# Rotation tables from angles, input weights built transposed in PSUM, scan states kept in PSUM

## The chip, the core and the metric

The kernel runs on one core of a Trainium2 chip. The metric is device time in microseconds (us) of one launch: 1091.52 us, the median of three runs (1089.41 to 1093.77). The engines are TensorE (PE; its weight loads are listed as PEld), VectorE (DVE), ScalarE (ACT), GpSimd (POOL) and SyncE (SP), which here only issues DMAs.

## The reference

Two encoder layers over 256 tokens of width 1024. Layer 0 mixes tokens with a state-space layer (S5), layer 1 with dilated attention; each then attends to 256 memory tokens and ends in an MLP. The change touches S5 alone: 64 groups of 16 channels, 64 complex states each, two directions.

```python
dt = exp(log_dt);  mag = exp(lam_re * dt);  ang = lam_im * dt
abar = mag * (cos(ang) + i sin(ang));  f = (abar - 1) / lam
bu  = einsum('bsgc,gpc->bsgp', u, f * b)                 # input into the states
x_t = abar * x_(t-1) + bu_t                              # scan over 256 tokens, both ways
y   = Re(einsum('bsgp,gcp->bsgc', x, c)) + d * u         # read out, then gelu and a GLU
```

Beside it stand the memory projections, `rms_norm(mem) @ w_kv` for both layers, which need nothing from S5.

## The kernel before, in words

Four tokens make one step, so a scan has 64 steps with the factor abar^4. The 64 groups go in eight chunks of eight. A chunk's states are 128 partitions (direction, state) by 512 columns (group, step), in one PSUM bank for the real part and one for the imaginary.

`s5_load`, `s5_params`, `s5_tables`, `s5_b`, `s5_turns`, `s5_c`, `s5_input` and `s5_skip` are the pre-phase. It ends with the powers of abar (`tav`, `taq`), the transposed input `u2` and the rotations e^(i k theta) as a product of two small tables. Then `s5` runs the chunks:

- `s5_weigh_in` (L1019): six DVE products make the input weights V (L1027 to L1029), PE transposes them (L1034), ACT copies them out (L1036).
- `turn` (L1056): six POOL products (L747 to L750) make the chunk's rotation table T.
- `drive` (L1065): 32 small matmuls (64 in the trace, two passes each) put V times u into the two state banks (L1073).
- `scan` (L1079): on DVE, rotate by T (six instructions from L1088), run the real recurrence (L1097), rotate back (six from L1100). ACT copies the states to SBUF (L1108, L1109).
- `impulse` (L1124): PE builds a kernel for the four tokens of one step (L1136, L1141), which goes through DRAM and back as M (L1146, L1152, both on ACT's queue).
- `weigh_out` (L1111): six POOL products make the output weights W.
- `read` (L1155): PE multiplies states by W and inputs by M (L1162, L1164); gelu (L1166); transposes (L1170); split into two halves (L1173 on ACT, L1174 on DVE).

In chunk ch the code puts weigh-in and drive of ch+1, scan of ch, impulse of ch, read of ch-1, weigh-out of ch+1. The memory projections (`memory_part`, `gemm32`, L241) are written after `s5`, but the scheduler that builds the program lays the instructions of each engine in one fixed order, and fits them in where its model of the engines has room. Each engine runs its own order strictly. The weights of the projections (`raw`, four buffers) are loaded on SP's queue, which is also in order.

After S5 come the last memory projection, which uses weights split into high and low halves (L154 on ACT, L155 on DVE, L200 to L202 on PE), the GLU and the other stages.

Of the kernel before, what the change touches and what calls it, by code (L numbers as in the profile page):

```python
# [17 lines left out]
P = 128  # L18
D = 1024
KT = 8  # L20
S = 256
DFF = 4096
EPS = 1e-6
NEG_INF = -1e30
XH = 4
# [36 lines left out]
class Trunk:  # L62
# [18 lines left out]
    @contextmanager  # L81
    def banks(self, na, nb):

        with self.tc.tile_pool(name="pa", bufs=na, space=PSUM) as self.pa, \
                self.tc.tile_pool(name="pb", bufs=nb, space=PSUM) as self.pb:
            yield
# [11 lines left out]
    def psb(self):  # L98
        return self.pb.tile([P, 512], F32, tag="B", name="psb")

# [651 lines left out]
    def s5_params(self, pr):  # L752
# [21 lines left out]
        v.tensor_scalar(n, th, 1.0 / (2 * math.pi), 12582912.0, op0=ALU.mult, op1=ALU.add)  # L774
        v.tensor_scalar(n, n, 12582912.0, None, op0=ALU.subtract)
# [5 lines left out]
        v.tensor_scalar(th, th, 3.1415925, -3.1415925, op0=ALU.min, op1=ALU.max)  # L781
        sn, hs, cs = nt(), nt(), nt()
        nc.scalar.activation(sn, th, AF.Sin)
        last = nc.scalar.activation(hs, th, AF.Sin, scale=0.5)
        self.exp_ln(last)
        v.tensor_tensor(hs, hs, hs, op=ALU.mult)
        v.tensor_scalar(cs, hs, -2.0, 1.0, op0=ALU.mult, op1=ALU.add)
        self.disc = (nt, mag, sn, cs)

    def s5_tables(self, ph):  # L790

# [3 lines left out]
        nt, mag, sn, cs = self.disc  # L795
# [3 lines left out]
        def table(name, l, copy=v.tensor_copy):  # L799
            ps = self.psb()  # L800
# [6 lines left out]
        e, q1, q2 = nt([G, 2, 2, 64]), nt(), nt()  # L807
        src = (cs, sn)
        for i in range(2):
            v.tensor_tensor(q1, src[1], src[1], op=ALU.mult)  # L810
            v.tensor_tensor(q2, src[0], src[0], op=ALU.mult)
            v.scalar_tensor_tensor(e[:, 1], src[0], 2.0 if i == 0 else -2.0, src[1], op0=ALU.mult, op1=ALU.mult)
            v.tensor_tensor(e[:, 0], q2, q1, op=ALU.subtract)
            src = (e[:, 0], e[:, 1])
# [3 lines left out]
        self.te = table("te", [e[:, 0], e[:, 1], r4])  # L818
# [16 lines left out]
        av, aq = nt([G, 2, 4, 2, 64]), nt([G, 2, 4, 2, 64])  # L835
# [5 lines left out]
        self.tav = table("tav", rows(av))  # L841
# [16 lines left out]
    def s5_load(self, pr, mem, craw):  # L858
# [19 lines left out]
        self.gb = pr.tile([64, D], F32, tag="gb", name="gb")  # L878
        nc.sync.dma_start(self.gb, a["norm_mix"][0].partition_broadcast(64))
# [9 lines left out]
    def s5_b(self, ph):  # L889
# [6 lines left out]
        for ri in range(2):  # L896
            for c0 in (0, 8):
                ps = self.psb()
# [5 lines left out]
    def s5_c(self, ph, pr):  # L904
# [4 lines left out]
        for c0 in (0, 8):  # L909
            pss = []  # L910
            for ri in range(2):
                ps = self.psb()
# [8 lines left out]
    def s5_skip(self, ph, pr):  # L921

        nc, a = self.nc, self.a
        G = 64
        dn = pr.tile([G, 16], F32, tag="dn", name="dn")
        nc.sync.dma_start(dn, a["s5_d"][0].rearrange("(g c) -> g c", c=16))
        dr = pr.tile([G, 8, 16], F32, tag="dr", name="dr")
        nc.gpsimd.tensor_copy(dr, dn.unsqueeze(1).to_broadcast([G, 8, 16]))
        ps = self.psb()
        nc.tensor.transpose(ps[:, :G], dr.rearrange("g a c -> g (a c)"), self.ident[:G, :G])  # L930
        dc = pr.tile([P, 16], F32, tag="dc", name="dc")
        for j in range(4):
            nc.vector.tensor_copy(dc[32 * j:32 * j + 32, :], ps[32 * j:32 * j + 32, j:G:4])
# [22 lines left out]
    def s5_input(self, ph):  # L956
# [7 lines left out]
        for q in range(4):  # L964
            t = xs[q % 2]
            cs = slice(q * 256, (q + 1) * 256)
            for s in range(4):
                nc.vector.scalar_tensor_tensor(t[:, :, 0, s], self.xraw[s][:, cs].rearrange("k (g c) -> k g c", c=16),
                                               r[:, s:s + 1], self.gb[:, cs].rearrange("k (g c) -> k g c", c=16),
                                               op0=ALU.mult, op1=ALU.mult)  # L970
            nc.scalar.copy(t[:, :, 1].rearrange("k g s c -> k g (s c)"), t[:, :, 0].rearrange("k g s c -> k g (s c)"))
            for b in range(2):
                ps = self.psb()
# [4 lines left out]
                nc.scalar.copy(u[:, g0:g0 + 8, 1:65], ps.rearrange("p (g k) -> p g k", g=8))  # L978
        self.u2 = u

    def s5_turns(self, ph, early, t):

        nc = self.nc
        G = 64
        t = t.rearrange("p (r w g b) -> p r w g b", r=2, w=2, g=G)

        e = ph.tile([P, 2, 3, 2, G], F32, tag="sq", name="sq")
        v, gp = nc.vector, nc.gpsimd
        v.tensor_copy(e[:, :, 0, 0, :], self.te[:, 0:2, :])
        for i in range(5):  # L990
            (r, i0), (ro, io) = ([e[:, q, k % 3, k // 3, :] for q in range(2)] for k in (i, i + 1))
            x, y = (ph.tile([P, G], F32, tag="sqt%d" % q, name="sqt") for q in range(2))
            v.tensor_tensor(x, r, r, op=ALU.mult)
            v.tensor_tensor(y, i0, i0, op=ALU.mult)
            v.tensor_tensor(ro, x, y, op=ALU.subtract)
            v.scalar_tensor_tensor(io, r, 2.0, i0, op0=ALU.mult, op1=ALU.mult)
        fl = lambda x: x.rearrange("p w g b -> p (w g) b")
        gp.memset(t[:, 0, :, :, 0:1], 1.0)
        gp.memset(t[:, 1, :, :, 0:1], 0.0)
        for st in range(3):  # L1000
            m = 1 << st
            eb = [e[:, q, st].rearrange("p w g -> p (w g)").unsqueeze(2).to_broadcast([P, 2 * G, m]) for q in range(2)]

            def tmp():
                x = early.tile([P, 512], F32, tag="pt8", name="pt", bufs=2)
                return x[:, :2 * G * m].rearrange("p (g m) -> p g m", m=m)

            self.cmul(gp if st == 2 else v, [fl(t[:, q])[:, :, m:2 * m] for q in range(2)], [fl(t[:, q])[:, :, 0:m] for q in range(2)],
                      eb, tmp)
        return t  # L1010
# [8 lines left out]
    def s5_weigh_in(self, early, ch):  # L1019

        nc, v = self.nc, self.nc.vector
        V = early.tile([P, 8, 2, 4, 16], F32, tag="V", name="V")
        (ar, ai), (br, bn) = ([f(x, ch, ri) for ri in range(2)] for f, x in ((self.pwb, self.tav), (self.bcb, self.bb)))
        for o, (x0, y0, x1, y1, op) in ((V[:, :, 0], (ar, br, ai, bn, ALU.add)),
                                        (V[:, :, 1], (ai, br, ar, bn, ALU.subtract))):
            t0, t1 = self.tmp(early, 8, 4, 16), self.tmp(early, 8, 4, 16)
            v.tensor_tensor(t0, x0, y0, op=ALU.mult)  # L1027
            v.tensor_tensor(t1, x1, y1, op=ALU.mult)
            v.tensor_tensor(o, t0, t1, op=op)  # L1029
        VT = early.tile([P, 8, P], F32, tag="VT", name="VT", bufs=1)  # L1030
        for q in range(2):
            ps = self.psb()
            for j in range(4):
                nc.tensor.transpose(ps[:, j * P:(j + 1) * P],  # L1034
                                    V[:, 4 * q + j].rearrange("p r s c -> p (r s c)"), self.ident)
            nc.scalar.copy(VT[:, 4 * q:4 * q + 4, :], ps.rearrange("p (a b) -> p a b", a=4))  # L1036
        self.Vs[ch] = VT

    def s5(self, ph, early, turns, gT):
# [339 lines left out]
```

## Time and profile before

| | |
|---|---|
| median of three runs | 1091.52 us |
| the profiled execution | 1089.65 us |
| its span, first to last instruction | 1087.9 us |
| PE busy over the span | 1032.4 us (95%) |
| DVE, ACT, POOL busy | 723.2 (66%), 576.9 (53%), 223.0 us (21%) |
| granted PE clock, mean | 0.983 of full |

A busy share is a mean over stages with different limits. S5 takes about the first fifth of the span, so the share that matters for the change is that of its own stretches. The granted clock is in parts of 2.4 GHz; its lower level, 1.2 GHz, reads 0.5.

### The profile page before, as it was taken

To read this page: it belongs to the slowest core of one execution; us is meant where nothing else is said; L and a number is where in the kernel's file an instruction comes from. 1 tells how busy PE (TensorE), PEld (TensorE's weight loads), DVE (VectorE), ACT (ScalarE), POOL (GpSimd) and SP (SyncE) were. 2 spreads that over 40 slices of the span, in tenths; PEclk is the share of its full clock that TensorE was granted. 3 is DMA by queue.
4 is the path that set the end of the run, shared out by engine and by line. 5 is a ranking of instruction groups with operands and counts; after the bars stand their busy time and mean duration, and the time that the engine had idled before them with its cause. 6 is when DMAs were issued, how large, how long until landed. Compare 5 with 4: busy or idle time off the path is not lost. (4 is left out here: it accounts for less than half of the span.)

```text
span 1087.9 us, 16868 instructions
## 1 busy us (share of the span) xinstructions
PE 1032.4 (95%) x6526; PEld 847.5 (78%) x6526; DVE 723.2 (66%) x1101; ACT 576.9 (53%) x1026; POOL 223.0 (21%) x186
## 2 busy tenths in 40 slices
PE   4689899998999999999989999999999999999998
PEld 3445565566899899998868878878788989889996
DVE  7999998346678754445576776778836766454444
ACT  6254444375576654444445665667545656444443
POOL 3979985011000010011040030000200000100000
PEclk8799999998999999999999999999999999999999
DMA  8313223255552456655566556554434435556552
GB/s 200 86 54 108 64 76 115 90 178 176 178 175 102 134 179 190 190 180 190 177 193 174 169 159 182 162 156 137 134 116 155 136 116 168 185 174 196 188 187 104
DMA packets 98428, 164.04 MB, mean 151 GB/s; under 512 B 16640, under 2 KB 27052, under 8 KB 98092
## 3 DMA queue, kind: packets, MB, share of 16 engines
q1 hardware_dynamic: 89052, 159.10, 47.7%
q10 hardware_dynamic: 9296, 3.87, 1.4%
q8 instruction: 51, 0.84, 0.3%
q14 instruction: 29, 0.24, 0.1%
HBM read 160.96 MB, written 3.83 MB: 151 GB/s over the span
## 5 line engine op out<-in xcount | busy, mean ns | idle before, releaser
L155 DVE TENSOR_TENSOR wlo<-raw,whi 128x1024 fp32r<-128x1024 f32 x264 | 329.9, 1250 | 238.5 <-ACT whi L154 235.0
L154 ACT CAST whi<-raw 128x1024 fp32r<-128x1024 f32 x264 | 276.7, 1048 | 226.5 <-PE psa L202 142.0
L200 PE MATMUL psa<-whi,xs 128*128 128x512 f32 x448 | 177.6, 397 | 0.5 <-ACT sg L1204 0.5
L202 PE MATMUL psa<-whi,xs 128*128 128x512 f32 x448 | 176.7, 394 | 0.0
L201 PE MATMUL psa<-wlo,xs 128*128 128x512 f32 x448 | 176.3, 393 | 0.0
L285 POOL TENSOR_TENSOR sq<-rl 128x512 f32<-128x512 f32 x32 | 40.1, 1252 | 534.2 <-ACT rl L284 534.2
L272 PE MATMUL psb<-xs,whi 128*128 128x256 f32 x512 | 145.1, 283 | 0.0
L274 PE MATMUL psb<-xs,whi 128*128 128x256 f32 x512 | 145.0, 283 | 0.0
L276 PE MATMUL psb<-xs,wlo 128*128 128x256 f32 x512 | 144.9, 283 | 0.0
L202 PE MATMUL psa<-whi,hl 128*128 128x512 f32 x256 | 101.5, 397 | 0.0
L201 PE MATMUL psa<-wlo,hh 128*128 128x512 f32 x256 | 101.5, 397 | 0.0
L200 PE MATMUL psa<-whi,hh 128*128 128x512 f32 x256 | 101.4, 396 | 0.0
L272 PEld LDWEIGHTS psb<-xs,whi 128*128 128x128 f32 x512 | 98.2, 192 | 0.9 <-DVE xs L177 0.4
L274 PEld LDWEIGHTS psb<-xs,whi 128*128 128x128 f32 x512 | 98.2, 192 | 0.5
L276 PEld LDWEIGHTS psb<-xs,wlo 128*128 128x128 f32 x512 | 98.3, 192 | 0.0
L200 PEld LDWEIGHTS psa<-whi,xs 128*128 128x128 f32 x448 | 84.3, 188 | 16.8 <-ACT sg L1204 0.9
L202 PEld LDWEIGHTS psa<-whi,xs 128*128 128x128 f32 x448 | 84.2, 188 | 16.5
L201 PEld LDWEIGHTS psa<-wlo,xs 128*128 128x128 f32 x448 | 84.3, 188 | 15.9
L241 PE MATMUL psa<-raw,mT 128*128 128x512 f32 x192 | 94.6, 636 | 0.0
L241 PEld LDWEIGHTS psa<-raw,mT 128*128 128x128 f32 x192 | 36.8, 203 | 38.5 <-issue 37.5
L202 PEld LDWEIGHTS psa<-whi,hl 128*128 128x128 f32 x256 | 48.2, 188 | 11.6
L201 PEld LDWEIGHTS psa<-wlo,hh 128*128 128x128 f32 x256 | 48.3, 189 | 11.1
(332 smaller groups left out, 1630.2 us busy)
## 6 DMA issues: line engine op xcount, KB each, us to landing
raw<-in_mlp_w SPq DMA_DIRECT2D x128, 512.0 KB, 4.3
raw<-in_attn_w_qkv SPq DMA_DIRECT2D x72, 512.0 KB, 3.8
raw<-in_xattn_w_kv SPq DMA_DIRECT2D x32, 512.0 KB, 4.0
raw<-in_s_w_glu SPq DMA_DIRECT2D x16, 512.0 KB, 4.6
raw<-in_xattn_w_q SPq DMA_DIRECT2D x16, 512.0 KB, 3.4
raw<-in_xattn_w_o SPq DMA_DIRECT2D x16, 512.0 KB, 3.6
raw<-in_attn_w_o SPq DMA_DIRECT2D x8, 512.0 KB, 4.4
bias_d<-bias_o SPq DMA_DIRECT2D x1, 1536.0 KB
```

Of the source, the lines that this page charges most:

```text
L154: self.nc.scalar.copy(hi, src)
L155: self.nc.vector.tensor_sub(lo, src, hi.bitcast(F32))
L200: nc.tensor.matmul(acc[t], xh[:, k0 + k, sl], hi[:, k % 2, :], start=st, stop=False)
L201: nc.tensor.matmul(acc[t], xh[:, k0 + k, sl], lo[:, k % 2, :], start=False, stop=False)
L202: nc.tensor.matmul(acc[t], xl[:, k0 + k, sl], hi[:, k % 2, :], start=False, stop=en)
L241: nc.tensor.matmul(acc[t], xT[:, k + q, t * P:(t + 1) * P], raw[:, q, :], start=k + q == 0, stop=k + q == KT - 1)
L272: nc.tensor.matmul(o, hi[:, k % 2, fs], xh[:, kt, :], start=st, stop=False, skip_group_check=True)
L274: nc.tensor.matmul(o, hi[:, k % 2, fs], xl[:, kt, :], start=False, stop=False, skip_group_check=True)
L276: nc.tensor.matmul(o, lo[:, k % 2, fs], xh[:, kt, :], start=False, stop=en, skip_group_check=True)
L285: nc.gpsimd.tensor_mul(sq, rl, rl)
```

## The change

1. *Rotations from angles.* `s5_params` also works out theta of a step, in turns and reduced (`nf`, seven DVE instructions). `s5_turn` makes a whole table T for one chunk from it: three products on DVE (chunks 0 and 1) or POOL (2 to 7), then one Abs and two Sin on ACT. All eight tables are made in the pre-phase and kept, in the space of `h`, `k1`, `k0` and one slot. `s5_turns` and `turn` go.
2. *Input weights.* The powers `av` are written to DRAM with their negative. For each chunk eight DMAs read them back into A, each row to 16 partitions. ACT spreads b over the four tokens (E, two halves), PE transposes E into PSUM, and one DVE product per half, PSUM times A, gives both parts of V with the contraction over all 128 partitions. `drive` uses them so.
3. *States.* The second rotation ends in the PSUM banks; ACT copies from there in four pieces of 64x512.
4. *Input.* ACT scales x by the row norm and writes it twice; the gain is applied when DVE takes the transposes out of PSUM.
5. *Banks.* The pool of accumulators has two banks instead of three, the common pool two instead of five, and the states get four of their own.

```diff
+    def s5_turn(self, early, T, ch, eng):
...
+        eng.tensor_tensor(y, self.kn.unsqueeze(1).to_broadcast([P, 8, 64]),
+                          self.te[:, 1, 8 * ch:8 * ch + 8].unsqueeze(2).to_broadcast([P, 8, 64]), op=ALU.mult)
+        eng.tensor_scalar(n, y, MAGIC, MAGIC, op0=ALU.add, op1=ALU.subtract)
+        eng.tensor_tensor(T[:, 1], n, y, op=ALU.subtract)
+        nc.scalar.activation(T[:, 0], T[:, 1], AF.Abs)
+        nc.scalar.activation(T[:, 0], T[:, 0], AF.Sin, scale=-6.283185, bias=self.quarter)
+        nc.scalar.activation(T[:, 1], T[:, 1], AF.Sin, scale=-6.283185)
...
     def s5_weigh_in(self, early, ch):
...
+        A = self.A1 if ch % 2 else early.tile([P, 2, 8, P], F32, tag="A", name="A")
+        for q in range(8):
...
+            nc.sync.dma_start(A[16 * q:16 * q + 16].rearrange("c v g x -> c v (g x)"), src)
+        for h in range(2):
+            E = early.tile([P, 4, 2, 4, 16], F32, tag="E", name="E")
+            for ri in range(2):
+                nc.scalar.copy(E[:, :, ri], self.bcb(self.bb, ch, ri)[:, 4 * h:4 * h + 4])
             ps = self.psb()
             for j in range(4):
+                nc.tensor.transpose(ps[:, j * P:(j + 1) * P], E[:, j].rearrange("p r s c -> p (r s c)"),
+                                    self.ident)
+            nc.vector.tensor_tensor(V, ps.rearrange("p (g x) -> p g x", g=4).unsqueeze(1).to_broadcast([P, 2, 4, P]),
+                                    A[:, :, 4 * h:4 * h + 4], op=ALU.mult)
...
         def drive(ch):
...
-            S_ = [self.psb(), self.psb()]
+            S_ = [self.pss(), self.pss()]
...
-                                         VT[hs, j, 64 * d:64 * d + 64],
-                                         self.u2[hs, 8 * ch + j, 0:64] if d == 0 else
-                                         self.u2[hs, 8 * ch + j, 65:1:-1], start=True, stop=True)
+                                         V[j // 4][:, ri, j % 4, 64 * d:64 * d + 64],
+                                         self.u2[:, 8 * ch + j, 0:64] if d == 0 else
+                                         self.u2[:, 8 * ch + j, 65:1:-1], start=True, stop=True)
...
-            with k.banks(3, 5):
+            with k.banks(2, 2, 4):
...
+                        k.s5_turn(ph, Ts[0], 0, nc.vector)
+                        k.s5_turn(ph, Ts[1], 1, nc.vector)
                         k.s5_weigh_in(ph, 0)
                         k.s5_c(ph, pr)
+                        k.s5_skip(ph, pr)
                         k.s5_input(ph)
+                        for c in range(2, 8):
+                            k.s5_turn(ph, Ts[c], c, nc.gpsimd)
```

How the built order moves, at three places. First PE in the middle of the chunks, before: one chunk's gelu transposes, the next chunk's weight transposes and drive, and L241, the memory projections.

```order
L241 MATMUL psa<-raw,mT 128x512
L1170 MATMUL psb<-ident,G 128x64 x4
L1034 MATMUL psb<-ident,V 128x128 x8
L241 MATMUL psa<-raw,mT 128x512 x7
L1073 MATMUL psb<-u_487,VT 64x64 x32
L1136 MATMUL psb<-wk,bb 32x112 x8
```

The same place now (L1172 gelu transposes, L1047 weight transposes, L1077 drive, L1138 and L1143 impulse):

```order
L1172 MATMUL psb<-ident,G 128x64 x4
L1047 MATMUL psb<-ident,E 128x128 x8
L1077 MATMUL pss<-u_461,V 64x64 x32
L1138 MATMUL psb<-wk,bb 32x112 x8
L1143 MATMUL psb<-dd,ident 128x16
```

No projection matmul (now L249) stands between drive of chunk 0 and drive of chunk 7 any more: 16 of the 96 come ahead of the chunks, 80 after the last drive. In the trace each counts twice.

Second, SP's queue ahead of and in the chunks, before: weights of the projections.

```order
L227 DMA raw<-in_xattn_w_kv 128x2x512 x2
L926 DMA dn<-in_s_d 64x16
L476 DMA tb<-in_bias_table 32x24
L480 DMA junk<-in_bias_onehot 33x384
L227 DMA raw<-in_xattn_w_kv 128x2x512 x4
```

Now (`avd` is the DRAM copy of the powers; `A` and `v_91` are the two buffers of A):

```order
L235 DMA raw<-in_xattn_w_kv 128x2x512 x2
L858 DMA avd<-h 64x4x128 x4
L484 DMA tb<-in_bias_table 32x24
L488 DMA junk<-in_bias_onehot 33x384
L1039 DMA A<-avd 16x2x1024 x8
L1039 DMA v_91<-avd 16x2x1024 x8
```

Behind these come six more groups of eight reads, the gains and `h`, and only then the next weights.

Third, ACT in the pre-phase, before: squares of x, copies of b and the two small row norms.

```order
L951 ACTIVATE k_82,uss<-xs 64x1024 x2
L901 ACTIVATE bb<-psb 128x8x64
L130 ACTIVATE rs_l<-uss 64x4
L901 ACTIVATE bb<-psb 128x8x64
L131 ACTIVATE ur<-rs_l 64x4
```

Now, further on in the pre-phase, part of the tables (L1018 Abs, L1020 and L1021 Sin) with the norm of the memory (L138, L139) between:

```order
L1018 ACTIVATE k_87<-k_87 128x512
L138 ACT_TABLE_LOAD
L138 ACTIVATE rs_l<-ssv 128x2
L1020 ACT_TABLE_LOAD
L1020 ACTIVATE k_87<-k_87,quarter 128x512
L1021 ACTIVATE k_87<-k_87 128x512
L1018 ACTIVATE k_87<-k_87 128x512
L139 ACT_TABLE_LOAD
L139 ACTIVATE rmem<-rs_l 128x2
L1020 ACT_TABLE_LOAD
```

The two norms, which shared one function table, now change tables four times between Sin's; with those of the other norm ACT has seven loads after its first Sin where it had one. The copies of u, which ACT made at L971, are the 16 scalings of L987 now.

## Rows read from the trace of the kernel before

**Rows 1.** stretches, all engines: busy us (count), granted clock, DMA share, GB/s

```profile
0.00:67.00 67.00, 43.46 (x290) 29.17 (x291) 59.93 (x132) 32.20 (x64) 40.80 (x49) 0.82 0.54 132
67.00:189.00 122.00, 109.22 (x1108) 66.18 (x1112) 117.29 (x139) 55.82 (x105) 104.07 (x82) 0.97 0.28 84
189.00:230.00 41.00, 39.49 (x280) 22.70 (x270) 14.88 (x22) 15.91 (x28) 0.00 (x0) 1.00 0.27 79
230.00:300.00 70.00, 65.33 (x280) 52.23 (x281) 41.88 (x50) 45.73 (x85) 9.50 (x4) 0.95 0.61 197
```

**Rows 2.** line L1088 on DVE: ns min/median/max, first and last start

```profile
L1088 DVE TENSOR_TENSOR tmp<-psb,xs x8: 690/691/692, 67.0 to 189.6; 128x512 f32<-128x512 f32 x8
```

**Rows 3.** groups on DVE, 104-185 us: count, busy us, mean ns

```profile
L1029 DVE TENSOR_TENSOR V<-tmp 128x512 f32<-128x512 f32 x9 | 11.8, 1309 | 0.5
L1097 DVE TENSOR_TENSOR_SCAN psb<-R,psb 128x512 f32<-128x512 f32 x10 | 11.6, 1210 | 0.0
...
L1090 DVE TENSOR_TENSOR psb<-psb,xs 128x512 f32<-128x512 f32 x5 | 3.5, 700 | 0.5
...
L1174 DVE TENSOR_TENSOR xs<-psb,xs 128x256 fp32r<-128x256 f32 x4 | 1.6, 412 | 0.0
```

**Rows 4.** the matmuls of the memory projections on PE

```profile
L241 PE MATMUL psa<-raw,mT x192: 592/592/1220, 24.3 to 227.4; 128*128 128x512 f32 x192
```

**Rows 5.** PE in time order, 113-134 us: start us, length us

```profile
113.89 1.16 PE L1073 MATMUL psb<-u,VT 64*64 64x64 f32 x64 [2.13 <-DVE xs L1174]
114.98 0.61 PE L1136 MATMUL psb<-wk,bb 128*32 128x112 f32 x16
...
116.72 0.45 PE L1162 MATMUL psb<-W,xs 128*64 128x64 f32 x4
...
121.76 1.12 PE L241 MATMUL psa<-raw,mT 128*128 128x512 f32 x2
...
124.42 6.17 PE L241 MATMUL psa<-raw,mT 128*128 128x512 f32 x14
132.87 1.65 PE L1073 MATMUL psb<-u,VT 64*64 64x64 f32 x64 [2.27 <-DVE xt L1104]
```

**Rows 6.** ACT in order of time, 142 to 145 us

```profile
142.29 0.59 ACT L1166 ACTIVATE G<-psb 64x512 f32<-64x512 f32 x1 [2.22 <-PE psb L1164]
142.38 2.52 ACTq L1152 DMA_DIRECT2D M<-kd  x4
144.94 0.37 ACT L1173 CAST xs<-psb 128x256 fp32r<-128x256 f32 x1 [2.05 <-PE psb L1034]
```

**Rows 7.** ACT in order of time, at 10.6 us

```profile
10.57 0.84 ACT L175 ACTIVATE mT<-psb,gains 128x256 f32<-128x256 f32 x2 [0.94 <-DVE n L811]
```

**Rows 8.** groups on ACT by shape, 0 to 80 us

```profile
L175 ACT ACTIVATE mT<-psb,gains 128x256 f32<-128x256 f32 x16 | 6.1, 486 | 0.9 <-DVE n L811 0.9
L978 ACT COPY u<-psb 128x512 f32<-128x512 f32 x8 | 4.5, 584 | 6.2 <-PE psb L976 6.2
L951 ACT ACTIVATE k<-xs 64x1024 f32<-64x1024 f32 x4 | 4.2, 1052 | 0.0
L901 ACT ACTIVATE bb<-psb 128x512 f32<-128x512 f32 x4 | 4.0, 1030 | 0.0
...
L1129 ACT COPY wk<-W 64x384 f32<-64x384 f32 x3 | 1.5, 512 | 3.9 <-POOL W L1121 3.9
...
L783 ACT ACT_TABLE_LOAD x1 | 1.3, 1283 | 0.0
L1083 ACT COPY R<-te 128x512 f32<-128x512 f32 x2 | 1.3, 628 | 0.0
...
L1127 ACT COPY wk<-ct 128x256 f32<-128x256 f32 x2 | 0.8, 416 | 0.0
```

**Rows 9.** PE in order of time, where the next two stages begin

```profile
229.88 0.50 PE L200 MATMUL psa<-whi,mp 128*128 128x512 f32 x1 [1.51 <-ACT junk L483]
...
261.05 0.39 PE L200 MATMUL psa<-whi,xs 128*128 128x512 f32 x1
```

More of the change, by code (lines that the diff above doesn't have):

```diff
@@ L81, in banks @@
     @contextmanager
-    def banks(self, na, nb):
+    def banks(self, na, nb, ns=0):
         with self.tc.tile_pool(name="pa", bufs=na, space=PSUM) as self.pa, \
                 self.tc.tile_pool(name="pb", bufs=nb, space=PSUM) as self.pb:
-            yield
+            if ns:
+                with self.tc.tile_pool(name="ps", bufs=ns, space=PSUM) as self.ps:
+                    yield
+            else:
+                yield
     def exp_ln(self, after=None):
@@ L805, in table @@
             return o
[L807 to L814, printed above, removed]
         r4 = nt()
@@ L840, in s5_tables @@
         rows = lambda x: [x[:, ri, q] for ri in range(2) for q in range(4)]
-        self.tav = table("tav", rows(av))
+        dp = self.ctx.enter_context(self.tc.tile_pool(name="av", bufs=1, space=bass.MemoryType.DRAM))
+        self.avd = dp.tile([2, 2, 4, G, P], F32, name="avd")
+        nav = self.h[:G, 1, :512].rearrange("g (s x) -> g s x", s=4)
+        avf = av.rearrange("g r s d p -> g r s (d p)")
+        nc.scalar.mul(nav, avf[:, 0], -1.0)
+        to = self.avd.rearrange("v r s g x -> v r g s x")
+        for v_, r_, src in ((0, 0, avf[:, 0]), (0, 1, avf[:, 1]), (1, 0, avf[:, 1]), (1, 1, nav)):
+            nc.sync.dma_start(to[v_, r_], src)
         nr, den, f = nt(), nt(), nt([G, 2, 2, 64])
@@ L997, in s5_turns @@
[L997 to L1009, printed above, removed]
@@ L1010, in s5_turns @@
-        return t
+        self.kn = ph.tile([P, 64], F32, tag="kn", name="kn")
+        one = ph.tile([P, 64], F32, tag="one", name="one")
+        nc.vector.memset(one, 1.0)
+        nc.vector.tensor_tensor_scan(self.kn, one, one, -1.0, op0=ALU.mult, op1=ALU.add)
+        self.quarter = ph.tile([P, 1], F32, tag="quarter", name="quarter")
+        nc.vector.memset(self.quarter, math.pi / 2)
+    def s5_turn(self, early, T, ch, eng):
+        nc = self.nc
+        y, n = (early.tile([P, 512], F32, tag="pt%d" % q, name="pt", bufs=2).rearrange("p (g k) -> p g k", g=8)
+                for q in range(2))
+        eng.tensor_tensor(y, self.kn.unsqueeze(1).to_broadcast([P, 8, 64]),
[5 more added lines that the diff above has]
+        nc.scalar.activation(T[:, 1], T[:, 1], AF.Sin, scale=-6.283185)
@@ L1019, in s5_weigh_in @@
     def s5_weigh_in(self, early, ch):
[L1021 to L1029, printed above, removed]
@@ L1030, in s5_weigh_in @@
-        VT = early.tile([P, 8, P], F32, tag="VT", name="VT", bufs=1)
-        for q in range(2):
+        nc = self.nc
+        d = self.avd[:, :, :, :, :]
+        A = self.A1 if ch % 2 else early.tile([P, 2, 8, P], F32, tag="A", name="A")
+        step = 64 * P
+        for q in range(8):
+            src = bass.AP(tensor=d.tensor, offset=d.offset + q * step + 8 * ch * P,
+                          ap=[[0, 16], [8 * step, 2], [1, 8 * P]])
+            nc.sync.dma_start(A[16 * q:16 * q + 16].rearrange("c v g x -> c v (g x)"), src)
@@ L1175, in read @@
                                     op=ALU.subtract)
-        for step in (turn, drive, weigh_out):
+        for step in (drive, weigh_out):
             step(0)
```

133 lines of the change are left out of this document (62 added, 71 removed).

## The prediction

> **What bounds the kernel now.** I read the stretches first, then the DVE and PE rows of the chunks. Up to 189 us DVE is the engine that sets the pace: busy 59.9 of the first 67 us and 117.3 of the next 122 [rows 1]. The scans of chunks 0 and 7 begin at 67.0 and 189.6, so a chunk takes 122.6 / 7 = 17.5 us [rows 2]. PE is just as full there (109.2 of 122), but not with S5: between the small matmuls lie the projections, a stretch of 14 passes at a time, and PE waits for DVE only a little over 2 us before each drive [rows 5]. From 189 us DVE is nearly idle and PE is full [rows 1]: it finishes projections and the last reads, and the next stage's first matmul comes at 229.9 [rows 9]. From there on PE sets the time. So the question is when PE has done all it must do ahead of that matmul, and that depends on what lies beside what.
>
> **The order, and what it costs.** The 192 passes of L241 run from 24.3 to 227.4 us [rows 4], a dense pass every 6.17 / 14 = 0.44 us [rows 5]. That is 85 us of PE work, most of it now free beside DVE. In the new order 32 passes precede the chunks and 160 come after the last drive; during the chunks PE has nothing to fill its waits with. The weights could not come earlier anyway: they are queued on SP behind the reads of A for chunk 7, whose buffer is free only after chunk 5. I therefore work out three pieces: the start of the first scan, seven chunk periods, and what PE has left from the last scan's start.
>
> *First scan.* DVE loses much of its pre-phase, but ACT gains more, and the drive of chunk 0 is held by it: its matmuls stand among the transposes of the memory, whose two banks are freed by ACT's copies, and these stand in ACT's order behind all eight rotation tables and the copies of W. ACT begins that work at 10.6 us [rows 7]. Kept work [rows 8]: 12 copies of mT at 6.1 / 16 = 0.38, squares of x 4.2, b 4.0, squares of the memory about 2.3 (half as wide as those of x), power tables about 2: 17.1 us. New: 24 instructions of 128x512 for the tables at 0.63 = 15.1; seven table loads at 1.28 = 9.0; 16 scalings of x, priced like L978 at 0.58 = 9.3; six copies into E at 0.42 = 2.5; a negated copy 0.6; the norms under 1: 37.3. Then R 0.63 and 0.2, and wk 0.42 and 4 x 0.51: 3.3. Together 57.7, hence 68.3. I add 4 for waits (POOL makes six angles and then W of chunk 0, PE the transposes of u) and 2.5 for the drive: 75 us, 8 later than now. Without any wait it is 67 to 71; with POOL a few us slower, 82.
>
> On the loads the page and the rows differ. In this trace a load is 1.28 us and nothing else [rows 8]. The Trainium skill (ScalarE: Activation LUTs, What ACT_TABLE_LOAD costs) adds a drain of about 1.38 us to each switch; by it the seven would cost 9.7 us more and the total would be 1141. The trace does not bear the drain out, and I leave it out.
>
> *A chunk period.* DVE's own work falls. Now V takes six instructions of about 1.3 us next to POOL [rows 3]; in their place come two products of 1,024 elements with one operand in PSUM, 2.5 us at the rate of the rotations (0.70 for 512, started 0.60 apart). With the scan (12 x 0.60, 2 x 1.21 = 9.6) and the 0.41 of L1174 that is 12.5. But each pair of products stands directly ahead of its own scan, so the chain now goes through PE and ACT and back. From the end of the second product:
> - three quarters of a drive and a handover, 2.1. A drive is 64 passes; on 64x64 tiles it takes 1.16 [rows 5]. No row shows it over all 128 rows. Bounds are 1.16 below and, above, the read's four passes of 128x64 in 0.37, which make 5.9 for 64. I take 2.5, since two column halves can still run together as the four of the impulse row do.
> - impulse, 114.98 to 116.72 = 1.75, and read of the chunk before, 116.72 to 121.76 = 5.0 [rows 5]
> - gelu starts 0.15 later; from gelu's start to the cast is 2.65, because four DMA issues (2.52) stand between [rows 6]; they still do
> - cast 0.37, handover 0.15, L1174's counterpart 0.41, handover 0.15, two products 2.5. The product needs that copy: it frees the bank into which E's second half is transposed (the common pool has two banks).
>
> The sum is 15.3 at full clock. PE then has two waits per chunk, about 1 and 2.2 us. After a wait of 2.13 the drive took 1.16, after one of 2.27 it took 1.65, with the clock at its lower level [rows 5]. I add 0.3 for that: 15.6. The least is 13.5 (DVE's 12.5 and half a drive that it waits for), the most 24 (the 8.8 us of PE in the chain at 1.2 GHz). The reads of A stay hidden: eight issues at 2.52 / 4 = 0.63 [rows 6] are 5 us, and the buffer is free two chunks ahead; late reads would add up to 5 us per chunk.
>
> For the drive the Trainium skill (TensorEngine Tiling (Array Packing), Tiling Modes) allows four tiles at 64x64 and two at 128x64. By it 64 passes take 2.3 us, and the total would be 1 us less than mine; no row here shows it.
>
> *What PE has left.* From the start of the last scan: 160 passes x 0.44 = 70.4; reads of chunks 5, 6, 7, 15.1; impulse 1.75; the rest of the drive 1; three sets of gelu transposes about 1.4; bias matmuls and gain transposes about 2.5; four changes of accumulator at about 0.5, now that two banks hold just one pair: 94 us. Before, it was 229.9 - 189.6 = 40.3.
>
> *Sum.* 75 + 7 x 15.6 + 94 = 278 against 229.9: 48 us later. Some comes back. In 230 to 300 us PE has 4.7 us idle and a clock of 0.95, which is 3.5 lost over 70 us [rows 1], as key norms and weight splits on ACT come late; the next stage begins only 31.2 us after the last [rows 9]. These can now run beside the 70 us of projections. I give back 7 of 8.2. So +41 on the profiled 1089.65: 1131 us. (The median of three is 1.9 above the profiled execution, a small matter here.)
>
> **Rivals.**
> - *DVE alone counts* (the other side). If what ACT and PE gain lies hidden, the first scan could start near 40 us (ACT's 57.7 less the new 37.3, then drive) and the period be 12.5. That is 40 + 87.5 + 94 = 222, 8 us early, 15 with the later gain: 1075. It decides where the way from drive through read, gelu and cast is shorter than DVE's 12.5 and ACT is not the last of the pre-phase. For it: DVE is full now and loses a third of a chunk. Against: the sum of 15.3 holds no doubtful row but the drive, and the 94 us of tail remain.
> - *Gelu's DMA issues get out of the way*, and the pre-phase has no waits: 67 + 7 x 13.5 + 94 = 255.5, +25.6, less 8: 1107. For it: in one chunk PE waits less than in another, and ACT has room. Against: the issues follow gelu in the new order as well.
> - *The clock stays low in the chunks.* PE loses its filler; if the waits keep it at 1.2 GHz, the period is 24: 80 + 168 + 94 = 342, 112 later, less 7: 1195. For it: the drive at 132.87 [rows 5], and a clock of 0.82 in the first 67 us [rows 1], where PE has gaps. Against: a slower PE makes the gaps shorter, and after 2.13 us it was at full speed.
>
> **How the numbers follow.** The forecast has 0.62, its own range 1115 to 1152 (first scan 70 to 80, period 14.8 to 17, 3 to 8 us given back). The issues rival 0.18, the clock rival 0.11, both slower. DVE alone 0.06. Between these, no change, 0.03. A change of 0.5%, 5.5 us, is about what a measurement of this kernel can tell from none. So slower 0.91, same 0.03, faster 0.06. The range leaves out the first rival and most of the clock rival: 1100 to 1165.
>
> **What would show it.** Right: no L249 on PE between the first and the last drive; the first scan near 75 us with ACT busy before it; a period near 15.6 with DVE idle about 2.5 us per chunk, waiting for PE or for the cast; some 70 us of dense L249 behind the last scan's start; the next stage's first matmul (L208) near 278, its stretch shorter than 31.2. A drive row tells whether 2.5 was right. Wrong, if the first scan comes before 55 us or the period is under 13; if PE's clock in the chunks is near 0.5; or if the time is under 1100, which would mean that the tail of 94 us is not there.

## The result and the profile after

The changed kernel takes 1137.15 us (median of four runs, 1133.66 to 1139.9) against 1092.64 (1089.41 to 1096.59) in the same comparison: ratio 1.0404, 95% interval 1.0358 to 1.045. Forecast were 1131 us and a range of 1100 to 1165. The profiled execution took 1137.31 us, its span is 1135.5.

The stretches of the changed kernel, cut where the first scan begins, where the last one begins and where the next stage's first matmul begins, and then 70 us more (start and end, length, then busy us and count of PE, PEld, DVE, ACT, POOL; granted clock, DMA share, GB/s). They answer to [rows 1].

```profile
0.00:75.80 75.80, 46.56 (x253) 29.77 (x255) 36.46 (x87) 60.53 (x111) 51.81 (x56) 0.84 0.67 131
75.80:183.50 107.70, 79.17 (x1025) 64.12 (x1022) 86.45 (x118) 52.62 (x116) 41.26 (x37) 0.77 0.39 69
183.50:281.30 97.80, 94.89 (x395) 46.92 (x391) 17.65 (x27) 29.45 (x65) 3.75 (x2) 0.96 0.51 167
281.30:351.30 70.00, 69.53 (x313) 56.44 (x314) 42.18 (x50) 41.23 (x61) 4.73 (x2) 1.00 0.55 182
```

DVE has become light: 36 us of the first 76 and 86 of the 108 in the chunks. ACT is now the busiest engine ahead of the first scan, PE the full one behind the last. Over the chunks as a whole no engine is full, as one expects of a chain that goes from engine to engine.

The first, fifth, sixth and last start of a scan on DVE (start, length, in brackets the idle time before it and what ended it), answering to [rows 2]:

```profile
75.85 0.69 DVE L1092 TENSOR_TENSOR tmp<-pss,xs 128x512 f32<-128x512 f32 x1 [10.30 <-PE pss L1077]
...
134.87 0.69 DVE L1092 TENSOR_TENSOR tmp<-pss,k 128x512 f32<-128x512 f32 x1 [1.23 <-PE pss L1077]
151.23 0.69 DVE L1092 TENSOR_TENSOR tmp<-pss,k 128x512 f32<-128x512 f32 x1 [1.23 <-PE pss L1077]
...
183.47 0.69 DVE L1092 TENSOR_TENSOR tmp<-pss,k 128x512 f32<-128x512 f32 x1 [1.23 <-PE pss L1077]
```

So the first scan begins at 75.85 (forecast 75), and seven periods take 107.6 us, 15.4 each (forecast 15.6, before 17.5). PE around the last drive and behind it, and where the next two stages begin:

```profile
182.30 2.49 PE L1077 MATMUL pss<-u,V 128*64 128x64 f32 x44 [0.20 <-DVE V L1050]
...
191.03 1.75 PE L249 MATMUL psa<-raw,mT 128*128 128x512 f32 x2 [1.34 <-DMA raw<-in_xattn_w_kv]
...
203.18 8.85 PE L249 MATMUL psa<-raw,mT 128*128 128x512 f32 x20
...
224.05 54.90 PE L249 MATMUL psa<-raw,mT 128*128 128x512 f32 x126
281.28 0.50 PE L208 MATMUL psa<-whi,mp 128*128 128x512 f32 x1 [1.56 <-ACT k L335]
```

The projections stand there in one piece, 126 passes in 54.9 us, and the next stage's first matmul comes at 281.3 (forecast 278; before 229.9 [rows 9]). The gated projection begins at 303.9, 22.6 us later instead of 31.2, so 8.6 us come back. It stands 42.9 us later than before, where the forecast had 41. From there to the end the one profile shows 831.6 us, that of before 826.8; the code there is the same, and the kernels below take 826 to 833 there, so I make nothing of these 5 us.

One chunk of the changed kernel, cut from PE, ACT and DVE between the scans at 134.87 and 151.23:

```profile
136.46 0.71 PE L1138 MATMUL psb<-wk,bb 128*32 128x112 f32 x16
...
138.28 0.45 PE L1164 MATMUL psb<-W,xs 128*64 128x64 f32 x4
...
143.43 0.59 ACT L1168 ACTIVATE G<-psb 64x512 f32<-64x512 f32 x1 [2.43 <-PE psb L1166]
143.50 2.93 ACTq L1154 DMA_DIRECT2D M<-kd  x4
...
146.46 0.37 ACT L1175 CAST xs<-psb 128x256 fp32r<-128x256 f32 x1 [2.44 <-DMA M<-kd]
...
146.86 0.71 ACT L1044 COPY E<-bb 128x256 f32<-128x256 f32 x2
146.87 0.42 DVE L1176 TENSOR_TENSOR xs<-psb,xs 128x256 fp32r<-128x256 f32 x1 [1.87 <-ACT xs L1175]
147.21 1.21 DVE L1050 TENSOR_TENSOR V<-psb,v 128x1024 f32<-128x1024 f32 x1
...
148.67 4.22 PE L1077 MATMUL pss<-u,V 128*64 128x64 f32 x64
148.78 1.23 DVE L1050 TENSOR_TENSOR V<-psb,v 128x1024 f32<-128x1024 f32 x1 [0.35 <-PE psb L1047]
```

The reader is to see the ring: impulse (L1138), read (L1164), gelu (L1168), four DMA issues (L1154), cast (L1175), DVE's copy (L1176), two products (L1050), and the next drive (L1077). The lines after [rows 5, 6] are the same ones in the same order; what is gone is the dense L241 between them.

### The profile page after: what moved, and what is told of

The parts are those of the page before. It is cut to its first block, busy times and chain, and to the rows that moved or that the text cites. A ratio compares the mean times of both kernels' runs of the same rounds, so it can differ in the third digit from the quotient of the medians.

```text
span 1135.5 us, 16919 instructions
## 1 busy us (share of the span) xinstructions
PE 1061.1 (93%) x6518; PEld 870.9 (77%) x6518; DVE 667.7 (59%) x1035; ACT 606.9 (53%) x1093; POOL 170.3 (15%) x148
## 5 line engine op out<-in xcount | busy, mean ns | idle before, releaser
L210 PEld LDWEIGHTS psa<-whi,xs 128*128 128x128 f32 x448 | 85.2, 190 | 16.8
L249 PE MATMUL psa<-raw,mT 128*128 128x512 f32 x192 | 92.2, 634 | 1.3 <-DMA raw<-in_xattn_w_kv 1.3
L249 PEld LDWEIGHTS psa<-raw,mT 128*128 128x128 f32 x192 | 36.9, 201 | 46.4 <-issue 39.7
```

What stands on the lines that cost most here:

```text
L210: nc.tensor.matmul(acc[t], xl[:, k0 + k, sl], hi[:, k % 2, :], start=False, stop=en)
L249: nc.tensor.matmul(acc[t], xT[:, k + q, t * P:(t + 1) * P], raw[:, q, :], start=k + q == 0, stop=k + q == KT - 1)
```

## The experiments

Every kernel ran beside the kernel before, whose median was 1092.55 to 1094.07 us in these comparisons; a ratio is taken within its own. "Next" is the start of the next stage's first matmul, "tail" its distance from the last scan's start; the period is the mean of seven; all from the profiled execution, in us.

| kernel | median | ratio, 95% interval | first scan | period | tail | next |
|---|---|---|---|---|---|---|
| before | 1092.64 | | 67.0 | 17.5 | 40.3 | 229.9 |
| changed | 1137.15 | 1.0404 (1.0358 to 1.045) | 75.9 | 15.4 | 97.8 | 281.3 |
| before_tail | 1140.86 | 1.0426 (1.0387 to 1.0465) | 69.9 | 17.7 | 91.9 | 285.5 |
| tables_only | 1146.88 | 1.0488 (1.0468 to 1.0508) | 72.2 | 16.8 | 105.1 | 295.0 |
| tables_vfirst | 1117.02 | 1.0217 (1.0189 to 1.0245) | 70.5 | 16.3 | 77.6 | 261.9 |
| tables_2 | 1084.82 | 0.9948 (0.9917 to 0.998) | 71.3 | 15.7 | 48.4 | 229.7 |
| ring | 1115.44 | 1.0211 (1.0167 to 1.0254) | 67.5 | 20.3 | 54.5 | 263.8 |
| ring_loads | 1107.59 | 1.0145 (1.0097 to 1.0193) | 65.2 | 19.6 | 54.8 | 257.5 |
| ring_v_ap | 1123.51 | 1.0278 (1.0243 to 1.0313) | 77.9 | 20.7 | 33.4 | 256.3 |
| fill | 1142.27 | 1.0459 (1.0433 to 1.0486) | 98.1 | 20.0 | 47.1 | 285.3 |
| fill_pre | 1168.83 | 1.0701 (1.0672 to 1.0731) | 113.3 | 20.9 | 44.6 | 303.9 |
| loads | 1143.40 | 1.0435 (1.0402 to 1.0468) | 73.7 | 15.8 | 104.5 | 288.8 |
| m_sync | 1160.98 | 1.0618 (1.0602 to 1.0634) | 75.8 | 19.7 | 93.9 | 307.7 |
| m_pool | 1136.39 | 1.0407 (1.038 to 1.0434) | 77.1 | 15.9 | 94.3 | 282.6 |

### Is it the place of the projections? before_tail

```diff
             for k in range(0, KT, 2):
+                late = not ahead
                 raw = ahead.pop(0) if ahead else self.weight_raw(w, k, c)
...
+                with ExitStack() as st:
+                    if late:
+                        st.enter_context(self.tc.issue_after(self.drv.ins))
...
```

Here `self.drv` is the last matmul of the last drive, and the four matmuls of a weight stand inside the `with`.

> The kernel before, with nothing changed but the order of the projections on PE: those whose weights are not loaded ahead come behind the last drive, so that 16 of the 96 matmuls stand ahead of the chunks, none between the drives and 80 after, as in the changed kernel. Theory (the place of the projections makes the whole loss, and what the rest of the change gains and costs cancels): first scan 67, period 17.5 as before since DVE sets it, and 59 matmuls of 0.88 = 52 us more behind the last scan; 8 come back in the next stage: 1137 us, as the changed kernel. Rival (the change's other costs, ACT's pre-phase above all, make a good part of the loss): below 1120. Second rival (PE's clock falls between the drives and PE then sets the period): above 1145.

Measured 1140.86 us, within 4 us of the changed kernel. Its stretches, cut as above:

```profile
0.00:69.90 69.90, 45.72 (x288) 31.61 (x289) 59.74 (x132) 33.84 (x67) 43.01 (x52) 0.85 0.53 127
69.90:193.60 123.70, 85.20 (x1019) 66.90 (x1020) 119.36 (x140) 51.01 (x95) 102.42 (x79) 0.57 0.08 23
193.60:285.50 91.90, 90.40 (x365) 45.14 (x363) 17.71 (x27) 29.80 (x64) 3.75 (x2) 1.00 0.48 144
```

DVE still sets the period, 119 of 124 us, and the tail is 91.9 where 92 was worked out. PE's clock drops to a mean of 0.57 in the chunks, but PE has so much time there that the period hardly moves. The order of one group of matmuls, with nothing else of the change, loses as much as the whole change (the first scan came 2.9 us later, which the theory had not). The second sentence of that theory holds too: against this kernel the change is later by 6 us at the first scan, 16 us faster in seven periods and 6 us longer in the tail, which nearly cancels.

### Which part moves them? tables_only and tables_vfirst

tables_only takes the six-instruction weights, V transposed and VT copied by ACT, from the kernel before, and drops the powers in DRAM and the reads of A; all else is the change. tables_vfirst adds:

```diff
-    self.kvw = [self.weight_raw(w_kv, k, 0) ...]
+    self.kvw = [self.weight_raw(w_kv, k, D) ...]
-    k.memory_part(0, 0, kv[0][0], mT[:1], mr, k.kvw)
-    k.memory_part(0, 1, kv[0][1], mT[:1], mr)
+    k.memory_part(0, 1, kv[0][1], mT[:1], mr, k.kvw)
+    k.memory_part(0, 0, kv[0][0], mT[:1], mr)
```

> The change without its second part: rotation tables by Sin, states in PSUM and the bank pools stay, the input weights of the state space are again built by DVE in six instructions, transposed, and copied by ACT; no powers in DRAM, no reads of A. SP's queue has four weights of the projections ahead of the chunks again, but the projections' results go to buffers that hold the tables of chunks 4 to 7, so in the order PE still has none between the first and the last drive. Theory (the tail of projections makes the loss, and either part alone brings it): first scan 72 to 76, period 16 to 17.5 by DVE, tail about 95, so 1135 to 1150 us. Rival (the loss comes from the reads of A, which keep the weights back): about 1092, as before the change.

> As tables_only, and the projection whose result goes to the memory's buffer, which holds no table, is made first. In the order 48 of the 96 matmuls now stand ahead of or between the chunks' drives and 48 after (16 and 80 in tables_only). Theory (what stands after the last drive counts in full): 32 matmuls of two passes at 0.44 us fewer in the tail, 28 us less than tables_only if the chunks hide them, 20 to 28 in all. Rival (PE's work in the chunks lengthens the period by as much): within 5 us of tables_only.

Both times came out by the theory or close to it: 1146.9 (with a tail of 105 where about 95 was worked out), and 29.9 less, where 20 to 28 were. So there are two locks on the projections. That the second, the home of the tables, holds alone is shown by these two runs; that the first would is argued from one row. The first is the one the prediction named: SP's queue in the changed kernel (start, time from first to last issue):

```profile
162.39 8.45 SPq L1039 DMA_DIRECT2D v<-avd  x8
...
183.88 0.39 SPq L1243 DMA_DIRECT2D h<-in_x  x1
184.31 28.12 SPq L235 DMA_DIRECT2D raw<-in_xattn_w_kv  x7
```

The fifth weight is issued at 184.31, behind the last reads of A, the gains and h. The four before it feed 16 matmuls, so the other 80 had to come behind the last drive, wherever their results go. It is the order of this queue that holds them, not the reads as such: in fill (below) the loads are written among the reads of A, and 52 matmuls stand between the first and the last scan. The second lock is in the tables' home, as ACT's rows of the changed kernel show:

```profile
185.91 0.69 ACT L335 ACTIVATE k<-psa,rmem 128x512 f32<-128x512 f32 x1
...
197.11 0.69 ACT L335 ACTIVATE k<-psa,rmem 128x512 f32<-128x512 f32 x1 [0.40 <-DVE pss L1107]
```

The first pair of results goes to the buffer that holds the tables of chunks 6 and 7. The second of them waits for DVE's L1107, the last scan's use of its table, and until then it occupies one of the two banks that are left for the projections. In tables_only four more weights are issued by 66.2 us, but the first pair of results leaves its two banks only at 198.8 and 214.2, behind the last scan's start at 189.9. Whether a third bank alone would have helped was not tried.

### More freedom for the order: tables_2

As tables_vfirst, with the projection into k1 second and that into k0 last, and with the two edits of loads (below).

```diff
-    k.memory_part(0, 0, kv[0][0], mT[:1], mr)
     k.memory_part(1, 0, kv[1][0], mT[1:], mr)
+    k.memory_part(0, 0, kv[0][0], mT[:1], mr)
```

> As tables_vfirst, with the projection into k1 (tables of chunks 4 and 5) second and the one into k0 (6 and 7) last, and the norms and function tables as in loads. In the order 65 of the 96 matmuls stand ahead of the last drive, 31 after (48 and 48 in tables_vfirst). Theory: 17 x 0.88 = 15 us fewer in the tail, first scan 2 us earlier: 1100 us. Rival (PE is full in the later chunks, and their period grows by what the tail loses): 1110 to 1115.

It did better than the theory: 1084.82 us (ten runs, 1081.88 to 1093.91), 0.5% faster than before, the interval just clear of one. Its stretches and, from 90 to 185 us, DVE's groups (count, busy us, mean ns), answering to [rows 3]:

```profile
0.00:71.30 71.30, 45.13 (x290) 28.96 (x291) 48.37 (x99) 51.25 (x99) 44.01 (x48) 0.89 0.50 120
71.30:181.20 109.90, 101.41 (x1114) 64.76 (x1114) 99.40 (x139) 54.12 (x110) 52.91 (x45) 0.95 0.27 79
181.20:229.70 48.50, 47.46 (x262) 25.80 (x260) 14.85 (x22) 21.33 (x56) 0.00 (x0) 1.00 0.39 121
229.70:253.50 23.80, 23.04 (x96) 17.71 (x97) 16.66 (x15) 17.62 (x26) 10.42 (x4) 1.00 0.70 216
```

```profile
L1031 DVE TENSOR_TENSOR tmp<-tav,bb 128x512 f32<-128x512 f32 x10 | 8.0, 797 | 0.2
L1032 DVE TENSOR_TENSOR tmp<-tav,bb 128x512 f32<-128x512 f32 x10 | 7.7, 774 | 0.0
L1033 DVE TENSOR_TENSOR V<-tmp 128x512 f32<-128x512 f32 x10 | 6.9, 692 | 1.4 <-PE psb L1038 0.9
```

The six instructions that took 1.31 us each [rows 3] take 0.69 to 0.80: POOL, busy 104 of 122 us in the chunks before, is busy 53 of 110, since it no longer builds a table per chunk. That this is POOL's doing fits the trace of before itself: of these instructions from 60 us on, the eight beside an idle POOL take 0.68 us on average, the 30 beside a POOL that is busy over nine tenths of their time 1.45. The period is 18.8 in the first chunk, where POOL is still busy throughout, 14.0 to 14.7 in the next four, and 16.6 and 17.4 when PE fills up late. Against tables_vfirst the tail lost 29 us where 15 were worked out: besides the 17 matmuls, PE is idle 1 instead of 6 us there and at clock 1.00 instead of 0.89. The next stage begins at 229.7, as before the change, and is 7 us shorter, which is the gain. How much of the step from tables_vfirst is the order's and how much that of the two norms is open: they were changed together, but the first scan, where the norms should tell, came no earlier (71.3 against 70.5).

### Tables made chunk by chunk: ring, ring_loads, ring_v_ap

```diff
-    for c in range(2, 8):
-        k.s5_turn(ph, Ts[c], c, nc.gpsimd)
...
     self.s5_weigh_in(early, ch + 1)
+    self.s5_turn(early, Ts[(ch + 1) % 2], ch + 1, gp)
     drive(ch + 1)
```

ring and ring_loads are made of tables_only, ring_v_ap of the whole change, with the reads of A on POOL's queue.

> As tables_only, but the rotation table of a chunk is made in the chunk before (three instructions on POOL, three on ACT) in two buffers in turn, so that no table lies in a buffer that a projection writes, and 18 of the 24 table activations leave the pre-phase. In the order 61 of the 96 projection matmuls stand ahead of the last drive, 35 after (16 and 80 in tables_only). Theory: first scan 72.2 - 18 x 0.63 = 61; period 16.3 as in tables_only and tables_vfirst; from the last scan 66 us (77.6 in tables_vfirst less 13 x 0.88): 61 + 114 + 66 = 241, some 1093 us, level with before. ACT changes its function table twice a chunk, 2.6 us, for which it has room. Rival (PE is full again in the chunks, and the period goes back to 17.5): 1101. Second rival (the loads stand in the way from gelu to the cast): period 19, 1112.

> As ring, with both norms ahead of the first Sin of the tables and the table of Ln and Exp loaded once, as in loads. Theory (ACT sets the first scan): up to five loads of 1.28 us fewer, 3 to 6 us less than ring, about 1089. Rival (with 18 activations gone, PE's transposes of u or DVE's weights set the first scan): same as ring.

> The whole change with the tables made chunk by chunk as in ring_loads, and the reads of A issued by POOL instead of SP, so that neither the tables' buffers nor the reads of A keep the projections back. In the order nearly all 96 projection matmuls now stand ahead of the reads of chunk 0, none after the last drive. Theory (PE's work is what counts, wherever it stands): 80 matmuls of 0.88 us leave the tail, which shrinks from 98 to about 28, the first chunks come up to 40 us later, the period stays at 15 to 16: 115 for the second scan, 6 x 15.5, 28: 236, about 1093 us. Rival (the period is a chain through gelu that the order cannot hide, and POOL's eight issues per chunk lengthen it to 18): 115 + 6 x 18 + 28 = 251, about 1107.

The first scan came to 67.5 and 65.2, not to 61 and below, and the tail to 54.5, shorter than worked out; but the period went to 20, and the times came out near the second rival of ring (1112). ACT in ring, in the chunk of the scan at 161.4:

```profile
163.59 1.28 ACT L1012 ACT_TABLE_LOAD   x1
...
166.52 1.28 ACT L1157 ACT_TABLE_LOAD   x1
171.81 0.59 ACT L1157 ACTIVATE G<-psb 64x512 f32<-64x512 f32 x1 [4.00 <-PE psb L1155]
...
181.83 1.28 ACT L1012 ACT_TABLE_LOAD   x1
```

The two loads per chunk are there, but the second lies in a wait for PE, so the time is near that rival's, but its cause is not shown. Three of ring's seven periods are long (23.8, 26.0 and 22.0; the others 16.8 to 18.0), and in those PE is the busiest engine: 23.8 of 23.8 and 22.0 of 22.0 us in the two that hold 26 passes of the projections, 24.0 of 26.0 in the one that holds none, with the granted clock at its lower level (0.50). That is nearer to the first rival, PE full, with the clock on top; why the clock stayed there is open. ring_v_ap tells more: with 93 matmuls ahead of the reads of chunk 0 the first two periods are 28.6 and 29.8, the rest 15.7 to 19.1, and the tail shrinks to 33. It is 14 us faster than the change (rival: 1107; measured 1123), a third of the loss, and the tables and the queue of the reads were changed with it. Of the 64 us that leave the tail, the first two periods take back 31 (they hold 110 passes), the other five 7, the first scan 2, and the next stage 8: it is 30.6 us long instead of 22.6.

### Matmuls inside the chain: fill and fill_pre

```diff
             if ch < 6:
                 impulse(ch)
+            for _ in range(PER[ch]):      # 2 or 3 weights, 8 to 12 matmuls
+                next(fill, None)
             if ch > 0:
                 read(ch - 1)
```

> The changed kernel with the projections written into the chunk loop: two or three weights (8 to 12 matmuls of two passes) per chunk between impulse and read, first the projection into the memory's buffer, which holds no table; the tables of chunks 2, 3 go to k0, 4, 5 to k1, 6, 7 to h. In the order 24 of the 96 matmuls stand ahead of the chunks, 56 to 60 between the first and the last drive, 16 after. Theory (PE's work is the bound as soon as there is something to put between the drives, and its clock comes back with it): period 18 us (PE 11 and 8 x 0.88), drives at 2.4 instead of 3.5 to 4.2, last scan to next stage 38 instead of 98: 77 + 7 x 18 + 38 = 241, 40 earlier, about 1097 us. Rival (the matmuls stand in the chain and lengthen it by all of their 7 us): 77 + 7 x 22.4 + 38 = 272, about 1128.

> As fill, with eight weights instead of four written ahead of the chunks: 40 matmuls stand ahead of the last part of the first drive, 8 after the last. Theory (PE has over 20 us idle ahead of the first drive, where this costs little): 14 us fewer later, up to 5 more at the first scan: 9 to 14 us less than fill, about 1085 us. Rival (the transposes of u and of the memory wait behind these matmuls, and the first scan comes as much later): same as fill.

In fill_pre the second projection is written over the tables of chunks 2 and 3 ahead of their scans; the instructions are all there, and only its time is read. Neither theory gave the time; of fill's rival the period came true. PE in fill:

```profile
151.26 0.40 PE L1164 MATMUL psb<-dd,ident 128*128 128x16 f32 x2
151.50 7.11 PE L252 MATMUL psa<-raw,mT 128*128 128x512 f32 x16
...
164.34 0.46 PE L1193 MATMUL psb<-ident,G 64*128 64x64 f32 x4 [0.68 <-ACT G L1189]
164.73 0.66 PE L1068 MATMUL psb<-ident,E 128*128 128x128 f32 x4
166.59 1.11 PE L1068 MATMUL psb<-ident,E 128*128 128x128 f32 x4 [1.20 <-ACT E L1065]
```

Between impulse and read the 16 passes stand in the chain with their whole 7.1 us, and the waits behind gelu and E are still there: periods of 21.2 to 25.1 from chunk 2 on, 22.4 on average as the rival has it. On top of that the first scan came 22 us later, because I had moved the tables of chunks 2 and 3 to the buffer in which x is scaled, and POOL's angles waited for its last transposes. fill_pre put 15 us more ahead of the first scan (98.1 to 113.3) and took 2.6 from the tail: its rival, and worse. Filling helps only beside a wait. In tables_2 the order puts the passes between the two halves of V's transposes, where PE would wait for DVE, and the drive follows at once; DVE is busy 13.8 of the 14.2 us of that period:

```profile
106.95 0.66 PE L1038 MATMUL psb<-ident,V 128*128 128x128 f32 x4
107.44 5.32 PE L249 MATMUL psa<-raw,mT 128*128 128x512 f32 x12
112.59 0.60 PE L1038 MATMUL psb<-ident,V 128*128 128x128 f32 x4
113.12 1.44 PE L1067 MATMUL pss<-u,VT 64*64 64x64 f32 x64
```

### ACT's issues and function tables: m_sync, m_pool, loads

```diff
-    nc.scalar.dma_start(kd, ...)            # m_sync: nc.sync, m_pool: nc.gpsimd
-    nc.scalar.dma_start(m[16 * s_:...], src)
+    nc.sync.dma_start(...)
```

> The changed kernel, with the write of kd and the four reads of M (L1148, L1154) issued by SP instead of ACT. Theory (the chunk is a chain through gelu, and ACT's issues stand in it): the cast of the chunk after gelu and the copies into E's second half no longer wait for 2.5 to 2.9 us of issues, so both products of the next chunk come about 1.75 us earlier; period 15.4 to about 13.6 us, the last scan 10 to 11 us earlier, about 1126 us. Rival (DVE or PE sets the period, the issues lie beside it): period stays at 15.4, 1137. Second rival: on SP the reads of M stand behind reads of A that wait for a buffer, so M comes late and the read of a chunk waits for it: slower than 1137.

> The changed kernel, with the write of kd and the reads of M issued by POOL, which has no reads of A in its queue (on SP the same made the period 19 us, as M stood behind them). Theory (ACT's issues stand in the chain): period 13.6, about 1126 us. Rival: POOL's issues take longer or wait in order behind W, M comes late again: 1137 or more.

Neither shortened the period. In m_sync it is 19.7 (18.1 without the last one of 29.2), slower as the second rival said, but the other way round: the reads of A stand behind the reads of M, which wait for kd to land, and DVE waits for A:

```profile
162.04 2.36 DVE L1050 TENSOR_TENSOR V<-psb,v 128x1024 f32<-128x1024 f32 x2 [3.60 <-DMA v<-avd]
```

In m_pool the cast comes right behind the transposes, but now E's first copies stand behind it on ACT instead of ahead of gelu:

```profile
146.08 0.37 ACT L1175 CAST xs<-psb 128x256 fp32r<-128x256 f32 x1
146.67 0.71 ACT L1044 COPY E<-bb 128x256 f32<-128x256 f32 x2
148.18 0.71 ACT L1044 COPY E<-bb 128x256 f32<-128x256 f32 x2 [0.80 <-PE psb L1047]
```

The order changed with the queue, so the price of the issues alone is not settled: 15.9 us against 15.4 says only that taking them off ACT is not enough.

```diff
-    nc.scalar.activation(hs, th, AF.Sin, scale=0.5)
+    last = nc.scalar.activation(hs, th, AF.Sin, scale=0.5)
+    self.exp_ln(last)
...
+    mr = k.row_rstd(kv[0][1], "mem")
     k.s5_angles(ph)
...
-    mr = k.row_rstd(kv[0][1], "mem")
```

> The changed kernel, with the row norm of the memory worked out beside the norm of x, ahead of the tables, and the table of Ln and Exp loaded once after the first two Sin: two loads of a function table after the first Sin instead of seven. Theory (ACT alone sets the first scan): 5 x 1.28 = 6.4 us earlier, first scan at 69.5, about 1131 us. Rival (POOL is next: its W of chunk 0 was ready at 69.9 and its last angles waited for ACT for only 3.1 us): first scan at 72.5 to 73, about 1134. Third: POOL alone sets it: no change.

The first scan came 2.1 us earlier for 6.4 us of loads, near the rival by POOL. The total is no better (1143.4; 1136.9 to 1144.6): PE's clock was 0.75 in the chunks and 0.90 in the tail of its profile against 0.77 and 0.96, and the last period took 19.1 instead of 16.0. PE's instructions are the same; only when it waits has changed. Why the clock fell there is open.

## Why the prediction was right

The mechanism was the one that was told: the projections lose their place beside DVE and stand behind the last drive. That the sum came so close, 42.9 us at the gated projection against 41, is partly luck: inside the first scan and the period, errors of opposite sign cancel.

- *The tail* was forecast at 94 and is 97.8; before_tail shows that this one term, without the rest, makes the loss. PE is idle 2.9 us in it and its mean clock is 0.96, which costs 3.8 of its 95 busy us; neither stood in the sum. The 2 us for changes of accumulator did, and the 126 passes in one piece show no such gap.
- *Why the tail is there* was half told. The prediction said "The weights could not come earlier anyway: they are queued on SP behind the reads of A". That is so in the order as built, but tables_only has no reads of A and the same 80 matmuls in the tail. The home of the tables in the projections' destinations, with two banks instead of three for their results, is a second lock that it missed. It was not needed for the sum, but it is what one has to open to mend the kernel.
- *The first scan*, forecast at 75: 75.85. From 10.6 us to its last copy of mT at 75.3 ACT is busy 55.7 us, where 57.7 were added up, and idle 9.0, where 4 were: 5.2 of these go to PE's transposes of the memory at 13.7 us, which the forecast did not name, 1.75 to POOL's W. The drive then costs 0.5 and not 2.5, since most of it runs beside that last copy. The 16 scalings took 10.3 us and not 9.3; seven loads of 1.28 came as counted. In loads, of 6.4 us taken from ACT 2.1 arrived, so POOL follows closely. The sum of one engine gave the right time, but it is not a price for every instruction in it.
- *The period*, forecast at 15.3 + 0.3: 15.4 on average, but not seven alike. The sum has impulse and read in every period; the first two hold no read (the first no impulse either), take 13.3 and 14.2, and DVE is busy 12.0 us of each. The five that hold one take 16.0 on average, 16.4 in the chunk shown. By parts of that chunk, forecast and measured: from the second product to impulse 2.1 and 2.82; impulse 1.75 and 1.82; read and the step to gelu 5.15 and 5.15; gelu to cast 2.65 and 3.03; to the products 1.08 and 0.75; products 2.5 and 2.80. The largest miss is the clock, which goes to and fro between its two levels with a mean of 0.77: the drive takes 3.5 to 4.2 us from the second chunk on. PE is then busy 12.3 to 14.2 us of a period of 15.2 to 16.3, so it is itself not far from full there.
- *The drive*, 2.5: in the first chunk, first row below, 60 passes took 2.37 us at a mean clock of 0.80. At full clock, in ring_v_ap, second row, 64 passes take 2.08 us; at the lower level the changed kernel's take 4.0 to 4.2:

```profile
74.36 2.37 PE L1077 MATMUL pss<-u,V 128*64 128x64 f32 x60
...
105.24 2.08 PE L1078 MATMUL pss<-u,V 128*64 128x64 f32 x64
```

So 2.5 was too much at full clock and too little at the clock that the chunks had. The estimate of 2.3 by the Trainium skill (TensorEngine Tiling (Array Packing), Tiling Modes), half as many tiles as at 64x64, is nearer to the 2.08.

- *The loads without a drain*: the trace bears it out, against the Trainium skill (ScalarE: Activation LUTs, What ACT_TABLE_LOAD costs). A load begins 0.02 us after the activation before it, and the next activation 0.01 after the load:

```profile
46.73 0.20 ACT L138 ACTIVATE rs_l<-ssv 128x2 f32<-128x2 f32 x1
46.95 1.28 ACT L1020 ACT_TABLE_LOAD   x1
48.24 0.72 ACT L1020 ACTIVATE k<-k,quarter 128x512 f32<-128x512 f32 x1
```

- *Given back*, 7: 8.6. before_tail has the same stage of 22.6 us, so it comes with the place of the projections; that the norms and splits of the next stage run beside them is the likely reason, and no run takes it apart.
- *The rivals.* DVE alone (1075) is out: the chain holds 15.4 where DVE's work is 12.3 (86.45 / 7). The clock rival came true in part, a mean of 0.77 and not 0.5. The rival of gelu's issues was tried twice and not reached.

## What to carry to other kernels

When a change shortens the engine that sets the pace, ask first what the other engines had laid beside it: here 118 of 192 passes, 52 us of PE, lost their place, and that alone made as great a loss as the whole change. Look for the place in the buffers that the change borrows: a table that lies in the destination of later work holds that work back, its PSUM banks with it, as surely as a full queue. And filling work pays where an engine waits, not wherever there is room in the count: 7.1 us of passes cost their full length in the chain, and 5.3 us of them lie hidden between two transposes.

## What the runs showed of the hardware

- An elementwise DVE instruction on 128x512 in SBUF took 1.31 us with POOL busy 85% of the time [rows 1, 3] and 0.69 to 0.80 with POOL busy 48% (tables_2); one by one in before, 0.68 beside an idle POOL and 1.45 beside a busy one. That is 6 x 0.55 = 3.3 us per chunk for DVE, where the new weights were to give it 7.9 - 2.5 = 5.4.
- PE's granted clock in the chunks was 0.97 with projections between the drives, 0.57 with the same instructions and the projections behind them (before_tail), 0.77 in the changed kernel, 0.95 in tables_2; in the tails it was 0.81 to 1.00, and 0.55 in that of ring_v_ap, which has no projections left.
- What waits in SP's queue holds up what stands behind it: in m_sync the write of kd, issued at 149.7 us when its source was ready, and four reads of M that waited for this write to land held up the last five of the eight reads of A for the next products, whose first three had gone at 137.8.
- A drive of 64 passes of 128x64 took 2.08 us at a granted clock of 1.00 (ring_v_ap) and 4.0 to 4.2 at 0.50 (the changed kernel); 64 passes of 64x64 took 1.16 [rows 5].
